# A decoder layer in fp32 on one core: three of eight blocks of the second FFN multiplied with seven products, with the sums of weights made during the first FFN

## The chip, the core and the metric

The kernel runs on one core of a Trainium2 chip. The metric is the device time of one execution in microseconds (us). Before the change the median of three timed runs is 2130.41 us (2130.28 to 2133.94).

## What is computed

The reference is one layer of a decoder trunk on 272 tokens (16 learned ones and 256 of the input), model width 2048, all in float32:

```python
h = h + 0.5 * swiglu(rms_norm(h), w_gate, w_up, w_down)      # first FFN, 5632 wide
u = rms_norm(h); z = u @ w_in                                # q, k, v, index q and k, conv, gates
h = h + (sigmoid(ga) * attention(z) + sigmoid(gc) * conv(z)) @ w_out
h = h + 0.5 * swiglu(rms_norm(h), w_gate2, w_up2, w_down2)   # second FFN, 5632 wide
return h[:, 16:]
```

`swiglu(x) = (silu(x @ w_gate) * (x @ w_up)) @ w_down`. Nearly all the work is matrix products with weights that are read once, about 390 MB in all.

## The kernel before, in words

**Float32 by three products.** Every operand is split into a high and a low part: ScalarE (ACT) writes `hi`, the value rounded to the matmul's type (`nc.scalar.activation(hi, raw, AF.Copy)`, L193), and VectorE (DVE) writes `lo = raw - hi` (L194). A product is hi·hi + hi·lo + lo·hi, so three matmuls. In the second FFN the three stand in `trio` (L431 to L433), 128 by 128 against 128 by 512. I call these three matmuls a trio. In the first FFN they are L397 to L399, 272 columns wide.

**The stream of weights.** The class `Stream` feeds all of it. A load is a DMA that SP issues into a raw buffer (L165). A step is a tile of at most 1024 columns that is split into `whi` and `wlo`; four pairs of these buffers exist, and `next()` hands the matmuls the oldest step after splitting three steps ahead (`AHEAD = 3`). The order of all engines is written out by the program: each call of `next()` runs the functions that are due. `st.put(fn, slot)` makes `fn` due slot // 2 steps later, before that step's split if the slot is even and behind it if it is odd. The table `LAG` holds those slots. `st.later(fn, lag)` does the same counted in whole steps.

**First FFN.** 264 steps, each of them 8 times 3 matmuls, at two steps per raw buffer of 2048 columns (1 MB).

**Second FFN.** Gate and up weights are cut into 11 column blocks f (groups of 6 and 5), each with eight depth blocks i of 2 by 2 sub-blocks; after each group of f, two passes d of the down projection follow, over 12 or 10 depth blocks. An ordinary block i is two steps "0" and "1" of four trios each. A mixed block computes the same 2 by 2 product with seven trios in place of eight (the Winograd form of Strassen's method), for four sums of weights (`t1` to `t4`, L214, four DVE operations of 128 by 512) and some sums of activations (`combos`, made once per operand). Before, blocks 2 and 5 of the eight are mixed (block 5 alone in the first f), and in the down passes blocks 5, 7, 9 of 12 and 5, 7 of 10. Its steps a, b, c, d (2, 2, 2 and 1 trios) are interleaved with the next block's steps, "a 0 b c 1 d", and the sums are made by DVE in between, in the raw buffers and in a tile `mix`. Raw loads of the second FFN go through a ring of six half buffers of 1024 columns (512 KB).

**What follows a block f.** The seven products lie in PSUM banks: four in `c` (one tile `three` of two banks, and `one`, `two`), four more in `m`, which is the other set of banks, and the next f swaps the two sets. After the last mixed block `spread` empties `m` (ACT L757, DVE L758 to L761); at the end of f `gather` empties `c` (DVE L771 to L773), `silu` (L779) and `times` (L786) make the gated value, `turn_gated` transposes 32 by 32 blocks (L658), `move_blocks` sends the tile to DRAM and back (POOL, L666 `hold<-mt` and four of L669 `mt<-hold`), and `split_blocks` writes the high and low part of `mid` (ACT L808, DVE L809), the operand of the down projection. Then `combos` prepares the sums of `mid` for a mixed block (L719 to L723, L705, L706). All these stand in the in-order queues of DVE and ACT between the splits of weights.

Of the kernel before, what the change touches and what calls it, by code (L numbers as in the profile page):

```python
# [15 lines left out]
P = 128  # L16
D = 2048
# [38 lines left out]
AHEAD = 3  # L56
WARM = 4, 4, 1
# [8 lines left out]
MIXED = 2, 5  # L66
FIRST_MIXED = 5,
MADE = ()
JOBS_FROM, JOBS_EVERY = 24, 7
DOWN_MIXED = {6: (5, 7, 9), 5: (5, 7)}  # L70
RAW = 2048
LEAD = dict(t3=3, t1=1, t2=3, t4=1)
LAG = dict(
    spread=(0, 0, 0, 0, 0), gather=(0, 2, 2), silu=(6, 6), times=(6, 8), turn=(11, 11), move=19, hi=(29, 27),
    lo=(29, 28), combos=(32, 32, 32, 32, 32, 32, 32, 37, 37), last_times=(6, 6), last_turn=(7, 7, 9, 9),
    last_split=14, half=(0, 3), drain=(8, 8, 12), act_combos=(6, 29, 30), factors=(10, 12, 14),
    out=(1, 2, 4, 16),
# [3 lines left out]
def order(n, mixed, made=()):  # L81

    out, i = [], 0
    while i < n:
        if i not in mixed:
            out += [(i, "0"), (i, "1")]
        else:
            a, b, c, d = [(i, x) for x in ("ABCD" if i in made else "abcd")]
            if i + 1 in mixed or i + 1 == n:
                out += [a, b, c, d]  # L90
            else:
                i += 1
                out += [a, (i, "0"), b, c, (i, "1"), d]
        i += 1
    return out


class Stream:
# [7 lines left out]
    def __init__(self, nc, raw_pool, split_pool):  # L106
        self.nc, self.raw_pool, self.split_pool = nc, raw_pool, split_pool
        self.loads, self.subs = [], []
        self.raw, self.ready = {}, {}
        self.n_loaded = self.n_split = self.at = 0  # L110
        self.blocks, self.waiting, self.steps = [], [], []
        self.first = []
        self.ring, self.n_ring, self.kept, self.done = [], 0, 0, set()

    def add(self, src, n, width, cuts=()):

        per = min(SUB // width, SUB // P)
        g = len(self.loads)
        self.loads.append((src, n * width, cuts, 2))
        at = [0, *cuts, n] if cuts else [*range(0, n, per), n]  # L120
        for a, b in zip(at, at[1:]):
            view = lambda a=a, b=b: self.raw[g][:, a * width : b * width]
            self.subs.append([view, b - a, width, [g] if b == n else [], []])

    def add_part(self, name, src, made=None):

        def load(x):
            self.loads.append((x, x.shape[1], (), 1))
            return len(self.loads) - 1

        if name in "01ABCD":
            g = load({
                "0": lambda: src[:, :SUB], "1": lambda: src[:, SUB:], "A": lambda: src[:, HALF : 3 * HALF],
                "B": lambda: src[:, 3 * HALF :], "C": lambda: made[:, :SUB], "D": lambda: made[:, SUB:],
            }[name]())
            n = self.loads[g][1]
            self.subs.append([lambda: self.raw[g][:, :n], n // HALF, HALF, [g], []])
        else:
            at = len(self.subs)
            if name == "a":  # L140
                self.pair = load(src[:, :SUB]), load(src[:, SUB:]), at, {}
            one, two, start, own = self.pair
            view = lambda: self.part(self.raw[one], self.raw[two], name)
            self.subs.append([view, 1 if name == "d" else 2, HALF, [], []])
            for x in dict(a=(), b=("t1",), c=("t3", "t2"), d=("t4",))[name]:
                own[x] = max(start, at - LEAD[x])
                self.subs[own[x]][4].append((x, lambda x=x: self.sum_of(self.raw[one], self.raw[two], x)))
            own[name] = at
            if name == "d":
                self.subs[max(own["b"], own["t2"])][3].append(one)  # L150
                self.subs[max(own["a"], own["t4"])][3].append(two)

    def load_one(self, between=(), queues=()):
        src, n, cuts, slots = self.loads[self.n_loaded]
        if slots == 1:
            tile, half = divmod(self.n_ring, 2)
            if tile < RAW_BUFS and not half:
                self.ring.append(self.raw_pool.tile([P, RAW], F32, name="raw"))
            raw = self.ring[tile % RAW_BUFS][:, half * SUB : half * SUB + SUB]
            self.n_ring += 1  # L160
        else:
            raw = self.raw_pool.tile([P, RAW], F32, name="raw")
# [13 lines left out]
    def fill(self):  # L176
        while self.n_loaded < len(self.loads) and (
            sum(x[3] for x in self.loads[self.kept : self.n_loaded + 1]) <= 2 * RAW_BUFS
        ):
            self.load_one()  # L180

    def split(self, upto):
        nc = self.nc
        while self.n_split < min(upto, len(self.subs)):
            view, kk, width, done, sums = self.subs[self.n_split]
# [18 lines left out]
    def blocks_of(self, one, two):  # L204
        b12, b11, b22, b21 = (x[:, i * HALF : (i + 1) * HALF] for x in (one, two) for i in range(2))
        return b12, b11, b22, b21, *(self.mix[:, i * HALF : (i + 1) * HALF] for i in range(3))

    def sum_of(self, one, two, name):

        b12, b11, b22, b21, t3, t2, t4 = self.blocks_of(one, two)  # L210
        to, a, b, op = dict(
            t3=(t3, b22, b12, "sub"), t1=(b12, b12, b11, "sub"), t2=(t2, t3, b11, "add"), t4=(t4, b21, t2, "sub")
        )[name]
        getattr(self.nc.vector, f"tensor_{op}")(to, a, b)  # L214

    def part(self, one, two, name):

        return dict(a=two, b=one, c=self.mix[:, : 2 * HALF], d=self.mix[:, 2 * HALF :])[name]
# [18 lines left out]
    def next(self):  # L237

        if not self.blocks:
            self.run(self.first, self.at)  # L240
            if self.steps:
                self.steps.pop(0)()
            self.split(self.at + 1 + AHEAD)
# [18 lines left out]
def tile_decoder_layer(  # L262
# [53 lines left out]
    for n in GROUPS:  # L316
        for f in range(n):
            now = MIXED if gu else FIRST_MIXED
            sums = {i: scratch.tile([P, RAW], F32, name=f"made{gu + i}") for i in now if i in MADE}
            made += [(gu + i, x) for i, x in sums.items()]  # L320
            for i, name in order(8, now, MADE):
                st.add_part(name, wgu2[gu + i], sums.get(i))
            gu += 8
        for _ in range(2):
            for i, name in order(2 * n, DOWN_MIXED[n]):
                st.add_part(name, wd2[down + i])
            down += 2 * n
# [107 lines left out]
    def quads(c, m, x, mixed, n, after_mixed, tail=False, made=()):  # L435
# [5 lines left out]
        for i, name in order(n, mixed, made):  # L441
# [7 lines left out]
            else:  # L449
# [3 lines left out]
                unit = dict(a=(p3, p2), b=(p5, p1), c=(p7, p6), d=(p4,), A=(p1, p3), B=(p2,), C=(p5, p6), D=(p7, p4))  # L453
                unit = [(*p, b) for b, p in enumerate(unit[name])]
            plan.append((unit, i == max(mixed) and name in "dD"))
# [121 lines left out]
    def ffn_features():  # L577
# [3 lines left out]
        with tc.tile_pool(name="ffn1", bufs=2, reuse_waits="tile") as fp:  # L581
# [16 lines left out]
            def job(i, to, at):  # L598
# [18 lines left out]
            for at, (i, to) in enumerate(made):  # L617
                job(i, to, JOBS_FROM + at * JOBS_EVERY)
# [56 lines left out]
    def ffn_tokens():  # L675

        with ExitStack() as pools:
# [3 lines left out]
            st.mix = fp.tile([P, 3 * HALF], F32, name="mix")  # L681
# [12 lines left out]
            late["junk"] = lambda: u[:, 0]  # L694

# [56 lines left out]
            put((add_up, root, inverse), LAG["factors"])  # L752
# [23 lines left out]
            def silu():  # L776
                s = gate_of()
                return [
                    lambda j=j: nc.scalar.activation(s[:, j - 1], s[:, j - 1], AF.Silu, scale=rcol[:, 0, j - 1 : j])  # L779
# [69 lines left out]
            for g, n in enumerate(GROUPS):  # L849
                for f in range(n):  # L850
                    box = {}
                    x, c, m = banks()
                    if f == g == 0:
                        rest = [i for i in MIXED if i not in FIRST_MIXED]
                        for i, slot in zip((*FIRST_MIXED, *rest), LAG["act_combos"]):
                            put(act_combos(i), 9 * (slot,))
                    now = {i: mixed[i] for i in (MIXED if f or g else FIRST_MIXED)}
                    quads(c, m, lambda k, j, part: known(("act", k // 4), act_tokens(k, j, part)), now, 8, lambda m=m: put(spread(m), LAG["spread"]), made=MADE)
# [717 lines left out]
```

## Time and profile before

| | |
|---|---|
| timed runs, median (lowest to highest) | 2130.41 us (2130.28 to 2133.94) |
| profiled execution: its time, its span | 2132.07 us, 2130.30 us |
| granted clock of the core | 1.00 |
| TensorE (PE) matmul busy | 2118.7 us, 99% |
| VectorE (DVE) busy | 1465.6 us, 69% |
| ScalarE (ACT) busy | 1016.3 us, 48% |
| moved by DMA | 411.28 MB, mean 193 GB/s |
| second FFN, first to last matmul | 1419.2 to 2124.2 us |

Matmuls are pipelined, so their busy times overlap, and a PE that is 99% busy can still have places where one matmul starts late. Such places are seen by counting the matmuls in equal stretches, and in the waits of PE itself. A line of waits reads: engine and line that waited, what released it, total us, times, the longest one. In a line of groups the last field is the idle time of that engine just before these instructions. In a line of windows "x" is the number of instructions that run in the stretch.

### The profile page before, as it was taken

Reading aid. Unit: us, or ns where it says so; the run is one execution under the profiler, and the core shown is the slowest. Engines: PE = TensorE matmul, PEld = TensorE weight load, DVE = VectorE, ACT = ScalarE, POOL = GpSimd, SP = SyncE. Lnnn points to the kernel's source line nnn. Section 1 sums busy time; section 2 is a strip of 40 time slices with the busy share of each in tenths; the row PEclk is TensorE's granted clock in tenths of the full one; section 3 lists DMA queues with packets and bytes.
Section 4 is the critical chain, followed back from the end, with each engine's and each line's share of the span. In section 5 each row is a group of like instructions: output and inputs, shape, how many; then the busy total and the mean of one; then the engine's idle time right before and its main releaser. Section 6 shows DMA issues by size and latency. Waiting matters only on the chain.

```text
span 2130.3 us, 31646 instructions
## 1 busy us (share of the span) xinstructions
PE 2118.7 (99%) x12809; PEld 1903.1 (89%) x12809; DVE 1465.6 (69%) x1953; ACT 1016.3 (48%) x1273; POOL 45.8 (2%) x93
## 2 busy tenths in 40 slices
PE   9999999999999999999999999999999999999999
PEld 9999999999999998799988888888887888888787
DVE  7555544455555556677677477768898887888897
ACT  6444433344444445455544444455555555554553
POOL 0000000000000000000000000010000000000000
PEclk9999999999999999999999999999999999999999
DMA  7555545555555555445455555676676766576664
GB/s 265 188 178 178 178 178 178 178 178 178 179 178 179 178 176 176 171 159 171 160 186 195 197 186 197 220 251 192 221 228 196 225 214 191 190 235 219 216 200 157
DMA packets 80291, 411.28 MB, mean 193 GB/s; under 512 B 9488, under 2 KB 10256, under 8 KB 49680
## 3 DMA queue, kind: packets, MB, share of 16 engines
q1 hardware_dynamic: 74880, 393.52, 54.9%
q0 software_dynamic: 4688, 14.68, 2.1%
q8 instruction: 100, 1.64, 0.3%
q10 hardware_dynamic: 576, 1.05, 0.1%
q14 instruction: 47, 0.39, 0.1%
HBM read 400.30 MB, written 8.91 MB: 192 GB/s over the span
## 4 chain that ended last, share of the span: by engine, by line
PE 88%; issue 7%; DMA 3%; DVE 1%; ACT 1%; POOL 1%; SPq 0%; DVEq 0%; ACTq 0%; POOLq 0%
PE pd L398 4%; PE pd L399 4%; PE pd L397 4%; PE pu L397 4%; PE pg L397 4%; PE pu L398 4%; PE pg L398 4%; PE pg L399 4%; PE pu L399 4%; PE three L431 4%; PE three L433 4%; PE three L432 4%; PE pgt L427 3%; PE pgt L426 3%; PE pgt L425 3%
## 5 line engine op out<-in xcount | busy, mean ns | idle before, releaser
L194 DVE TENSOR_TENSOR wlo<-raw,whi 128x1024 fp32r<-128x1024 f32 (+1 forms) x749 | 909.4, 1219 | 587.2 <-ACT whi L193 581.5
L193 ACT ACTIVATE whi<-raw 128x1024 fp32r<-128x1024 f32 (+1 forms) x749 | 787.6, 1056 | 914.8 <-PE three L433 169.8
L397 PE MATMUL pd<-mid,whi 128*128 128x272 f32 x704 | 201.7, 286 | 0.0
L398 PE MATMUL pd<-mid,whi 128*128 128x272 f32 x704 | 201.7, 286 | 0.0
L399 PE MATMUL pd<-mid,wlo 128*128 128x272 f32 x704 | 201.7, 286 | 0.0
L397 PE MATMUL pu<-act,whi 128*128 128x272 f32 x672 | 192.6, 287 | 0.0
L399 PE MATMUL pu<-act,wlo 128*128 128x272 f32 x672 | 192.5, 287 | 0.0
L397 PE MATMUL pg<-act,whi 128*128 128x272 f32 x672 | 192.5, 286 | 0.0
L398 PE MATMUL pg<-act,whi 128*128 128x272 f32 x672 | 192.5, 286 | 0.0
L399 PE MATMUL pg<-act,wlo 128*128 128x272 f32 x672 | 192.5, 286 | 0.0
L398 PE MATMUL pu<-act,whi 128*128 128x272 f32 x672 | 192.5, 286 | 0.0
L431 PE MATMUL three<-whi,act 128*128 128x512 f32 x352 | 137.2, 390 | 0.9 <-DVE u L761 0.7
L433 PE MATMUL three<-whi,act 128*128 128x512 f32 x352 | 137.0, 389 | 0.0
L432 PE MATMUL three<-wlo,act 128*128 128x512 f32 x352 | 137.0, 389 | 0.0
L397 PEld LDWEIGHTS pd<-mid,whi 128*128 128x128 f32 x704 | 132.6, 188 | 0.0
L398 PEld LDWEIGHTS pd<-mid,whi 128*128 128x128 f32 x704 | 132.6, 188 | 0.0
L399 PEld LDWEIGHTS pd<-mid,wlo 128*128 128x128 f32 x704 | 132.6, 188 | 0.0
L397 PEld LDWEIGHTS pg<-act,whi 128*128 128x128 f32 x672 | 126.6, 188 | 0.0
L399 PEld LDWEIGHTS pu<-act,wlo 128*128 128x128 f32 x672 | 126.6, 188 | 0.0
L398 PEld LDWEIGHTS pg<-act,whi 128*128 128x128 f32 x672 | 126.6, 188 | 0.0
L398 PEld LDWEIGHTS pu<-act,whi 128*128 128x128 f32 x672 | 126.6, 188 | 0.0
L397 PEld LDWEIGHTS pu<-act,whi 128*128 128x128 f32 x672 | 126.5, 188 | 0.0
(333 smaller groups left out, 4296.8 us busy)
## 6 DMA issues: line engine op xcount, KB each, us to landing
raw<-in_wgu_dram SPq DMA_DIRECT2D x177, 512.0 KB, 5.0
raw<-in_wgu_dram SPq DMA_DIRECT2D x86, 1024.0 KB, 4.8
raw<-in_wd_dram SPq DMA_DIRECT2D x44, 1024.0 KB, 4.8
raw<-in_wd_dram SPq DMA_DIRECT2D x88, 512.0 KB, 5.0
raw<-in_wcv_dram SPq DMA_DIRECT2D x24, 1024.0 KB, 4.8
raw<-in_wgc_dram SPq DMA_DIRECT2D x24, 1024.0 KB, 4.8
raw<-in_wga_dram SPq DMA_DIRECT2D x24, 1024.0 KB, 4.9
raw<-in_wo_dram SPq DMA_DIRECT2D x16, 1024.0 KB, 4.8
```

The lines of the kernel that those rows point to most:

```text
L193: nc.scalar.activation(hi[:, :n], raw, AF.Copy)
L194: nc.vector.tensor_sub(lo[:, :n], raw, hi[:, :n].bitcast(F32))
L397: nc.tensor.matmul(ps, whi, xhi, start=first, stop=False)
L398: nc.tensor.matmul(ps, whi, xlo, start=False, stop=False)
L399: nc.tensor.matmul(ps, wlo, xhi, start=False, stop=last)
L425: nc.tensor.matmul(ps, xhi, whi, start=k + i == 0, stop=False)
L426: nc.tensor.matmul(ps, xhi, wlo, start=False, stop=False)
L427: nc.tensor.matmul(ps, xlo, whi, start=False, stop=k + i == n - 1)
L431: nc.tensor.matmul(ps, x(0), w[0], start=first, stop=False)
L432: nc.tensor.matmul(ps, x(0), w[1], start=False, stop=False)
L433: nc.tensor.matmul(ps, x(1), w[0], start=False, stop=last)
```

## The change

1. **Three mixed blocks.** Blocks 1, 3, 5 of the eight are mixed (3 alone in the first f). The down passes keep theirs.
2. **Sums made early.** For each of the 41 mixed blocks (31 of gate and up, 10 of down) a job in the first FFN loads the weights (POOL, 1 MB), makes the four sums in place on DVE, and stores the tile to DRAM (POOL, 1 MB). Jobs start at step 24 and follow each other every 5 steps; a job's four sums come 5 to 8 steps after its load was issued, its store 9 steps after. Three buffers hold the jobs; for the first three a one-column copy on DVE keeps the load from being issued earlier.
3. **New steps.** A mixed block is now steps A, B, C, D (2, 1, 2 and 2 trios). A and B come from three quarters of the weights (1536 columns), C and D from the stored tile (2048 columns). They are not interleaved with the next block. The sums, the tile `mix` and the ring of half buffers are gone.
4. **Raw loads** of the second FFN fill whole buffers of 2048 columns; three buffers as before, and one is free when all its steps are split.
5. **Five pairs of split buffers** in the second FFN, and four steps ahead.
6. **Other places** in `LAG`: `gather` at once (0, 0, 0), `silu` 1, `times` 2, `turn` 4, `move` 12, `hi` 27, `combos` from 29 to 36, the factors of the norm at 23 to 27, and others.

```diff
-MIXED = 2, 5
-FIRST_MIXED = 5,
-JOBS_FROM, JOBS_EVERY = 24, 7
+MIXED = 1, 3, 5
+FIRST_MIXED = 3,
+JOBS_FROM, JOBS_EVERY = 24, 5
 LAG = dict(
-    spread=(0, 0, 0, 0, 0), gather=(0, 2, 2), silu=(6, 6), times=(6, 8), turn=(11, 11), move=19, hi=(29, 27),
+    spread=(0, 0, 0, 1, 1), gather=(0, 0, 0), silu=(1, 1), times=(2, 2), turn=(4, 4), move=12, hi=(27, 27),
...
-            a, b, c, d = [(i, x) for x in ("ABCD" if i in made else "abcd")]
-            if i + 1 in mixed or i + 1 == n:
-                out += [a, b, c, d]
-            else:
-                i += 1
-                out += [a, (i, "0"), b, c, (i, "1"), d]
+            out += [(i, x) for x in "ABCD"]
...
+        if name in "0A":
+            self.own = load(src if name == "0" else src[:, HALF:]), name == "A" and load(made)
+        g = self.own[name in "CD"]
+        a, b = {"0": (0, 2), "1": (2, 4), "A": (0, 2), "B": (2, 3), "C": (0, 2), "D": (2, 4)}[name]
...
-        while self.n_loaded < len(self.loads) and (
-            sum(x[3] for x in self.loads[self.kept : self.n_loaded + 1]) <= 2 * RAW_BUFS
-        ):
+        while self.n_loaded < min(len(self.loads), self.kept + RAW_BUFS):
             self.load_one()
...
-            for _, fn in sorted(sums, key=lambda x: ("t3", "t1", "t2", "t4").index(x[0])):
-                fn()
...
-            hi = self.split_pool.tile([P, SUB], F32R, name="whi")
-            lo = self.split_pool.tile([P, SUB], F32R, name="wlo")
+            hi, lo = self.place()
...
             for i, name in order(2 * n, DOWN_MIXED[n]):
-                st.add_part(name, wd2[down + i])
+                st.add_part(name, wd2[down + i], sums.get(i))
...
                 def load():
                     box["x"] = fp.tile([P, RAW], F32, name="made", bufs=3)
-                    nc.gpsimd.dma_start(box["x"], wgu2[i])
+                    if at < JOBS_FROM + 3 * JOBS_EVERY:
+                        nc.vector.tensor_copy(box["x"][:, :1], ones[:, :1])
+                    nc.gpsimd.dma_start(box["x"], src)
...
+            st.more = [[fp.tile([P, SUB], F32R, name=f"{n}{i}") for n in ("whi", "wlo")] for i in range(MORE)]
+            st.ahead = AHEAD + MORE
```

The function `job` stood in the kernel before, with an empty list of blocks.

**How the order of DVE changes at the end of a block f of the second FFN.** Before, from the last rows of one f's `spread` (L758 to L761) to the `gather` (L771 to L773) and the first sum of weights (L214) of the next:

```order
L194 TENSOR_TENSOR wlo<-raw,whi 128x1024 x2
L758 TENSOR_TENSOR u<-one,u 128x512
L759 TENSOR_TENSOR u<-two,u 128x512
L760 TENSOR_TENSOR u<-three,u 128x512
L761 TENSOR_TENSOR u<-three,u 128x512
L194 TENSOR_TENSOR wlo<-raw,whi 128x1024
L706 TENSOR_TENSOR below<-few,below 128x3x128
L194 TENSOR_TENSOR wlo<-raw,whi 128x1024
L771 TENSOR_TENSOR few<-three,u 128x1024
L194 TENSOR_TENSOR wlo<-raw,whi 128x1024
L772 TENSOR_TENSOR u<-one,u 128x512
L214 TENSOR_TENSOR mix<-raw 128x512
```

The `spread` stands two splits ahead of the next `gather`, and sums of weights stand among the splits. The same place on DVE with the change; L722 to L725 are the `spread`, L735 to L737 the `gather`, L161 the split:

```order
L670 TENSOR_TENSOR below<-few,below 128x3x128
L722 TENSOR_TENSOR u<-one,u 128x512
L723 TENSOR_TENSOR u<-two,u 128x512
L161 TENSOR_TENSOR wlo<-raw,whi 128x1024
L724 TENSOR_TENSOR u<-three,u 128x512
L725 TENSOR_TENSOR u<-three,u 128x512
L161 TENSOR_TENSOR wlo<-raw,whi 128x1024 x2
L161 TENSOR_TENSOR wlo_14193<-raw,whi_14192 128x512
L735 TENSOR_TENSOR few<-three,u 128x1024
L736 TENSOR_TENSOR u<-one,u 128x512
L737 TENSOR_TENSOR u<-two,u 128x512
L161 TENSOR_TENSOR wlo<-raw,whi 128x1024
```

Four splits now stand between the two, and no sum of weights is left; the whole `gather` comes in one piece.

**SP's loads at the start of the second FFN**, before and with the change (`in_wo` is the weight of the projection ahead of it, `in_wgu` the gate and up weights, `made_74` the stored tile of the first job):

```order
L165 DMA raw<-in_wo_dram 128x2048 x16
L165 DMA raw<-in_wgu_dram 128x1024 x96
L165 DMA raw<-in_wd_dram 128x1024 x48
L165 DMA raw<-in_wgu_dram 128x1024 x80
L165 DMA raw<-in_wd_dram 128x1024 x40
```

```order
L137 DMA raw<-in_wo_dram 128x2048 x16
L137 DMA raw<-in_wgu_dram 128x2048 x3
L137 DMA raw<-in_wgu_dram 128x1536
L137 DMA raw<-made_74 128x2048
L137 DMA raw<-in_wgu_dram 128x2048 x5
L137 DMA raw<-in_wgu_dram 128x1536
L137 DMA raw<-made_75 128x2048
```

Equal half loads become whole ones, and a mixed block loads one and three quarters of what an ordinary one loads.

More of the change, by code (lines that the diff above doesn't have):

```diff
@@ L56 @@
 AHEAD = 3
+MORE = 1
 WARM = 4, 4, 1
@@ L65, with order @@
 HALF = 512
-MIXED = 2, 5
-FIRST_MIXED = 5,
-MADE = ()
-JOBS_FROM, JOBS_EVERY = 24, 7
+MIXED = 1, 3, 5
+FIRST_MIXED = 3,
+JOBS_FROM, JOBS_EVERY = 24, 5
 DOWN_MIXED = {6: (5, 7, 9), 5: (5, 7)}
 RAW = 2048
-LEAD = dict(t3=3, t1=1, t2=3, t4=1)
 LAG = dict(
-    spread=(0, 0, 0, 0, 0), gather=(0, 2, 2), silu=(6, 6), times=(6, 8), turn=(11, 11), move=19, hi=(29, 27),
-    lo=(29, 28), combos=(32, 32, 32, 32, 32, 32, 32, 37, 37), last_times=(6, 6), last_turn=(7, 7, 9, 9),
-    last_split=14, half=(0, 3), drain=(8, 8, 12), act_combos=(6, 29, 30), factors=(10, 12, 14),
-    out=(1, 2, 4, 16),
+    spread=(0, 0, 0, 1, 1), gather=(0, 0, 0), silu=(1, 1), times=(2, 2), turn=(4, 4), move=12, hi=(27, 27),
+    lo=(28, 28), combos=(29, 29, 32, 32, 33, 33, 36, 36, 36), last_times=(4, 6), last_turn=(8, 11, 14, 14),
+    last_split=16, half=(1, 5), drain=(1, 3, 3), act_combos=(4, 7, 26), factors=(23, 25, 27), out=(1, 2, 4, 17),
+    act_split=(6, 15, 31),
 )
-def order(n, mixed, made=()):
+def order(n, mixed):
     out, i = [], 0
@@ L112, in __init__ @@
         self.first = []
-        self.ring, self.n_ring, self.kept, self.done = [], 0, 0, set()
+        self.kept, self.done = 0, set()
+        self.more, self.turn, self.ahead = [], 0, AHEAD
     def add(self, src, n, width, cuts=()):
@@ L118, in add @@
         g = len(self.loads)
-        self.loads.append((src, n * width, cuts, 2))
+        self.loads.append((src, n * width, cuts))
         at = [0, *cuts, n] if cuts else [*range(0, n, per), n]
@@ L122, in add @@
             view = lambda a=a, b=b: self.raw[g][:, a * width : b * width]
-            self.subs.append([view, b - a, width, [g] if b == n else [], []])
+            self.subs.append((view, b - a, width, (g,) if b == n else ()))
     def add_part(self, name, src, made=None):
         def load(x):
-            self.loads.append((x, x.shape[1], (), 1))
+            self.loads.append((x, x.shape[1], ()))
             return len(self.loads) - 1
[L131 to L151, printed above, removed]
@@ L153, in load_one @@
-    def load_one(self, between=(), queues=()):
[L154 to L162, printed above, removed]
+        if name in "0A":
+            self.own = load(src if name == "0" else src[:, HALF:]), name == "A" and load(made)
@@ L163, in load_one @@
+        g = self.own[name in "CD"]
+        a, b = {"0": (0, 2), "1": (2, 4), "A": (0, 2), "B": (2, 3), "C": (0, 2), "D": (2, 4)}[name]
+        self.subs.append((lambda: self.raw[g][:, a * HALF : b * HALF], b - a, HALF, (g,) if name in "1BD" else ()))
+    def load_one(self, between=(), queues=()):
+        src, n, cuts = self.loads[self.n_loaded]
+        raw = self.raw_pool.tile([P, RAW], F32, name="raw")
         at = [0, *(c * P for c in cuts), n]
@@ L202, in split, with place @@
             self.fill()
[L204 to L218, printed above, removed]
+    def place(self):
+        if self.more:
+            self.turn = (self.turn + 1) % (SPLIT_BUFS + len(self.more))
+            if self.turn < len(self.more):
+                return self.more[self.turn]
+        return [self.split_pool.tile([P, SUB], F32R, name=n) for n in ("whi", "wlo")]
     def put(self, fn, slot):
@@ L242, in next @@
                 self.steps.pop(0)()
-            self.split(self.at + 1 + AHEAD)
+            self.split(self.at + 1 + self.ahead)
             self.run(self.waiting, self.at)
@@ L318, in tile_decoder_layer @@
             now = MIXED if gu else FIRST_MIXED
-            sums = {i: scratch.tile([P, RAW], F32, name=f"made{gu + i}") for i in now if i in MADE}
-            made += [(gu + i, x) for i, x in sums.items()]
-            for i, name in order(8, now, MADE):
+            sums = {i: scratch.tile([P, RAW], F32, name=f"made{gu + i}") for i in now}
+            made += [(wgu2[gu + i], x) for i, x in sums.items()]
+            for i, name in order(8, now):
                 st.add_part(name, wgu2[gu + i], sums.get(i))
@@ L324, in tile_decoder_layer @@
         for _ in range(2):
+            sums = {i: scratch.tile([P, RAW], F32, name=f"sums{down + i}") for i in DOWN_MIXED[n]}
+            made += [(wd2[down + i], x) for i, x in sums.items()]
             for i, name in order(2 * n, DOWN_MIXED[n]):
-                st.add_part(name, wd2[down + i])
+                st.add_part(name, wd2[down + i], sums.get(i))
             down += 2 * n
@@ L433, in trio, with quads @@
         nc.tensor.matmul(ps, x(1), w[0], start=False, stop=last)
-    def quads(c, m, x, mixed, n, after_mixed, tail=False, made=()):
+    def quads(c, m, x, mixed, n, after_mixed, tail=False):
         def of(k, j):
@@ L440, in quads @@
         plan, joined = [], []
-        for i, name in order(n, mixed, made):
+        for i, name in order(n, mixed):
             k = 2 * i
@@ L452, in quads @@
                 p5, p6, p7 = (m[5], s1), (m[6], s2), (m[7], s3)
-                unit = dict(a=(p3, p2), b=(p5, p1), c=(p7, p6), d=(p4,), A=(p1, p3), B=(p2,), C=(p5, p6), D=(p7, p4))
+                unit = dict(A=(p1, p3), B=(p2,), C=(p5, p6), D=(p7, p4))
                 unit = [(*p, b) for b, p in enumerate(unit[name])]
-            plan.append((unit, i == max(mixed) and name in "dD"))
+            plan.append((unit, i == max(mixed) and name == "D"))
         flat = [id(p[0]) for unit, _ in plan for p in unit]
@@ L596, in times, with job @@
                 nc.vector.tensor_mul(box["v"], box["v"], box["s"])
-            def job(i, to, at):
+            def job(src, to, at):
                 box = {}
@@ L615, in job @@
                 st.later(lambda: nc.gpsimd.dma_start(to, box["x"]), at + JOBS_EVERY + 4)
-            for at, (i, to) in enumerate(made):
-                job(i, to, JOBS_FROM + at * JOBS_EVERY)
+            for i, (src, to) in enumerate(made):
+                job(src, to, JOBS_FROM + i * JOBS_EVERY)
             two = [aux_tile(f"start{i}") for i in range(2)]
@@ L679, in ffn_tokens @@
             mid = fp.tile([P, 4 * GROUPS[0], 2, SEQ], F32R, name="mid")
-            st.mix = fp.tile([P, 3 * HALF], F32, name="mix")
             u = fp.tile([P, 4, 512], F32, name="u")
@@ L750, in add_up @@
                 nc.vector.tensor_add(sums[:, 0], sums[:, 0], sums[:, 2])
-            put((add_up, root, inverse), LAG["factors"])
+            put((add_up, root, lambda: (inverse(), written.add("rcol"))), LAG["factors"])
             def spread(m):
@@ L778, in silu @@
                 return [
-                    lambda j=j: nc.scalar.activation(s[:, j - 1], s[:, j - 1], AF.Silu, scale=rcol[:, 0, j - 1 : j])
+                    lambda j=j: nc.scalar.activation(s[:, j - 1], s[:, j - 1], AF.Silu, scale=known("rcol", rcol[:, 0, j - 1 : j]))
                     for j in (1, 2)
@@ L854, in ffn_tokens @@
                         rest = [i for i in MIXED if i not in FIRST_MIXED]
-                        for i, slot in zip((*FIRST_MIXED, *rest), LAG["act_combos"]):
-                            put(act_combos(i), 9 * (slot,))
+                        for i, *slots in zip((*FIRST_MIXED, *rest), LAG["act_combos"], LAG["act_split"]):
+                            put(act_combos(i), 5 * (slots[0],) + 4 * (slots[1],))
                     now = {i: mixed[i] for i in (MIXED if f or g else FIRST_MIXED)}
-                    quads(c, m, lambda k, j, part: known(("act", k // 4), act_tokens(k, j, part)), now, 8, lambda m=m: put(spread(m), LAG["spread"]), made=MADE)
+                    quads(c, m, lambda k, j, part: known(("act", k // 4), act_tokens(k, j, part)), now, 8, lambda m=m: put(spread(m), LAG["spread"]))
                     put(gather(x, c), LAG["gather"])
```

2 lines of the change are left out of this document (1 added, 1 removed).

## The prediction

> **What bounds the kernel now.** I read the page first, then the second FFN in equal stretches, the waits of PE, ACT and DVE there, the chain of waits, the groups by line, and the DMAs' times to landing.
>
> The page's parts 1 and 4, busy time by engine and the chain that ended last:
>
> ```profile
> span 2130.3 us, 31646 instructions
> PE 2118.7 (99%) x12809; PEld 1903.1 (89%) x12809; DVE 1465.6 (69%) x1953; ACT 1016.3 (48%) x1273; POOL 45.8 (2%) x93
> PE 88%; issue 7%; DMA 3%; DVE 1%; ACT 1%; POOL 1%; SPq 0%; DVEq 0%; ACTq 0%; POOLq 0%
> ```
>
> The chain is PE nearly throughout: the end moves when PE has fewer matmuls, or when places vanish where it waits. What a trio costs is seen in the chain by its pieces inside the second FFN, the first matmuls (L431) of two trios in a row:
>
> ```profile
> 1466.64 0.23 PE two L431
> 1467.32 0.23 PE three L431
> ```
>
> They start 0.68 us apart, 0.2267 us per matmul. In stretches (us, PE busy and matmuls, PEld, DVE, ACT, POOL, clock, DMA share, GB/s), the first FFN, the end of the projection ahead of the second FFN, the whole second FFN, and three pieces of it:
>
> ```profile
> 95.00:700.00 605.00, 605.00 (x4908) 605.00 (x4907) 315.58 (x380) 243.33 (x287) 0.32 (x1) 1.00 0.51 179
> 1350.00:1419.00 69.00, 69.00 (x306) 57.11 (x305) 43.74 (x56) 35.04 (x50) 8.43 (x15) 1.00 0.76 258
> 1419.60:2124.20 704.60, 699.24 (x3069) 574.72 (x3068) 596.07 (x726) 365.94 (x405) 29.70 (x54) 1.00 0.65 208
> 1620.00:1660.00 40.00, 38.75 (x169) 31.12 (x168) 35.29 (x46) 21.19 (x25) 0.56 (x1) 1.00 0.69 216
> 1720.00:1760.00 40.00, 40.00 (x178) 33.14 (x177) 31.17 (x33) 19.53 (x20) 0.00 (x0) 1.00 0.74 235
> 1960.00:2000.00 40.00, 38.17 (x166) 30.56 (x165) 35.09 (x47) 20.48 (x25) 0.56 (x1) 1.00 0.66 207
> ```
>
> Undisturbed, 40 us hold 178 matmuls; at the ends of the two groups of gate and up they hold 169 and 166, so 9 and 12 are missing, 2.0 and 2.7 us. By the program the second FFN has 1025 trios, 1025 x 0.68 = 697.0 us, and it takes 704.6: **7.6 us are lost in it.** What PE, and ACT ahead of it, wait for there:
>
> ```profile
> PE one L432 <- DVE wlo L194: 3.7, 7, 0.8
> PE three L431 <- DVE u L761: 1.1, 3, 0.4
> ACT whi L193 <- PE three L433: 224.1, 183, 2.3
> ACT mid L808 <- DMA mt<-hold: 30.4, 9, 4.8
> ACT whi L193 <- DMA raw<-in_wgu_dram: 0.8, 2, 0.6
> ```
>
> PE waits for a late split on DVE or for `spread`, never for DMA itself. The weights come in time: ACT waits 224 us for PE to free a buffer and 0.8 us for a raw load. But ACT also stands 30.4 us in all before the tile that returns from DRAM, with splits queued behind. The chain shows where this reaches PE:
>
> ```profile
> 1652.27 7.45 DMA hold<-mt
> 1660.25 1.64 POOL mt L669 x3
> 1661.88 5.45 DMA mt<-hold
> 1668.60 0.52 ACT mid L808
> 1674.79 1.22 DVE wlo L194
> 1677.97 0.69 DVE u L761
> 1678.80 0.47 PE three L431
> ```
>
> The tile lands at 1667, then splits, `combos` and `spread` follow on a DVE with no room left, and PE's first matmul of the down pass starts late.
>
> **Part by part.** *Fewer trios.* 31 mixed blocks of gate and up in place of 21: ten trios less, 30 matmuls, 10 x 0.68 = **6.8 us off PE**. This is certain as work; the rest decides whether it shows.
>
> *Sums leave the second FFN.* Groups by line on DVE in the second FFN, and the split in the first:
>
> ```profile
> L194 DVE TENSOR_TENSOR wlo<-raw,whi 128x1024 fp32r<-128x1024 f32 x261 | 316.2, 1221 | 55.5 <-ACT whi L193 51.0
> L214 DVE TENSOR_TENSOR mix<-mix,raw 128x512 f32<-128x512 f32 x31 | 21.5, 692 | 1.1
> L786 DVE SCALAR_TENSOR_TENSOR few<-u,rcol,few 128x512 f32<-128x512 f32 x22 | 16.2, 746 | 0.0
> L771 DVE TENSOR_TENSOR few<-three,u 128x1024 f32<-128x1024 f32 x11 | 13.4, 1218 | 0.0
> L772 DVE TENSOR_TENSOR u<-one,u 128x512 f32<-128x512 f32 x11 | 7.5, 684 | 0.0
> L194 DVE TENSOR_TENSOR wlo<-raw,whi 128x1024 fp32r<-128x1024 f32 x205 | 251.4, 1227 | 288.2 <-ACT whi L193 288.2
> ```
>
> 31 mixed blocks x 4 sums x 0.69 = 85 us leave a DVE that is busy 596 of 704.6; the ten new ones add 10 splits of 1024 and 10 of 512 columns, 10 x (1.22 + 0.68) = 19 us on DVE (less on ACT, which has 339 us free). So 596 - 85 + 19 = 530 us of 698, 76% instead of 85%. In a mixed pair DVE had 3 x 1.22 + 0.68 + 2.76 of sums + 2.45 = 9.5 us to do in 15 trios or 10.2 us; now 6.8 us. The seven late splits sit in those pairs, so I expect most to go. The three waits for `spread` (L761) go too: before, step d of block 5 came with only block 7's eight trios (5.4 us) ahead of the next f; now D has blocks 6 and 7 behind it, 10.9 us.
>
> *The round trip through DRAM.* It takes 16 us from the turn: 7.45 + 1.64 + 5.45 in the chain above and the issues between. The turn's own row:
>
> ```profile
> L658 DVE STREAM_TRANSPOSE mt<-few 128x512 f32<-128x512 f32 x18 | 11.7, 687 | 0.0
> ```
>
> Before, the turn is due at slot 11, behind a split that waits for 18 trios of the next f: 12.2 + 2.3 + 1.4 = 15.9 us, so the tile is back at 31.9. The first `hi`, slot 27, stands behind a split that waits for 41 trios: 27.9 + 1.1 = 29.0. ACT would wait 2.9 us; measured are 30.4 / 9 = 3.4, so the method holds. Now the turn ends 8 us after the end of f (on DVE 2.6 of `gather`, 1.2 of split, 1.5 of `times`, 1.2, 1.4), the tile is back at 24, and ACT reaches `hi` after 34 trios and a split, 23.1 + 1.1 = 24.2. The wait falls from 3.4 us to between 0 and 2.
>
> Together the 7.6 us lost shrink to between 0 and all of it. I take 2.6, nearer to the free end, since each named cause is eased: **5.0 us off**.
>
> *The same work in the first FFN.* 41 x 4 x 0.69 = 113 us go to DVE there, where it idles 288.2 of 605 us for ACT; a step is 605 / (4908 / 24) = 2.96 us of PE, holding 1.23 us of split and now four sums in five steps, 0.55. Cover remains: splits run three steps ahead, 8.9 us. POOL's queue gains 82 DMAs, 2 x 1.05 MB per 14.8 us, 142 GB/s on top of 179. What the engines can do, at the start of the program and later, in stretches:
>
> ```profile
> 15.00:20.00 5.00, 4.67 (x38) 4.46 (x38) 4.28 (x8) 4.45 (x11) 0.00 (x0) 1.00 1.03 428
> 17.00:23.00 6.00, 6.00 (x51) 6.00 (x50) 5.67 (x10) 6.00 (x15) 0.00 (x0) 1.00 0.94 367
> 150.00:156.00 6.00, 6.00 (x51) 6.00 (x50) 3.60 (x5) 2.52 (x4) 0.00 (x0) 1.00 0.52 175
> ```
>
> 428 GB/s were moved, above the 321 needed, and PE runs 51 matmuls in 6 us at 367 GB/s as at 175. So heavier traffic alone doesn't slow PE; I cost this part at nothing (if the cover fails, below). No load of 1 MB by POOL is in the trace; nearest are these issues (KB, median us to landing), and below them SP's raw loads in the second FFN:
>
> ```profile
> raw<-in_wgu_dram SPq DMA_DIRECT2D x86, 1024.0 KB, 4.8
> hold<-mt POOLq DMA_DIRECT2D x10, 512.0 KB, 7.4
> mt<-hold POOLq DMA_DIRECT2D x40, 128.0 KB, 5.3
> DMA to landing us min/median/max: 3.4/5.0/8.4
> ```
>
> Between 4.8 and 2 x 7.4 = 14.8 us, and the sums ask for it 5 steps, 14.8 us, after its issue. I take 7.4: nothing waits. The Trainium skill, page "DMA: Bandwidth & Descriptors", section "Bandwidth", gives 6.15 us for 1 MB issued from GpSimd; by that, too, the sum would keep a zero here.
>
> *Whole raw buffers.* A mixed and an ordinary block load 0.79 + 1.05 + 1.05 = 2.88 MB in 10.2 us: 283 GB/s, near the 258 at the end of the projection, where PE lost nothing. A buffer is free when its last step is split. The tightest one carries C and D of block 3: its buffer held C and D of block 1, whose last split ends 6.7 us after f began (`gather` 2.6, splits 2 x 1.22, `times` 1.5, and 0.2). Issue 0.5 and landing 4.8 make 12.0; PE needs C after 26 trios, 17.7 us, less 2.3 for its two halves of the split: 15.4. So 3.4 us are left, and the load may take 8.2 us. Waits of ACT for raw will appear; PE should not see them.
>
> *Fifth pair of buffers, other slots of the norm's factors and of the first `combos`:* nothing, since ACT and DVE have time; the fifth pair is what keeps C and D, short steps, ahead.
>
> **Sum.** The profiled execution took 2132.07 us, 1.77 around its span of 2130.30; the median of the timed runs, 2130.41, lies 1.66 below. I work on the span and put the difference onto the median: -6.8 - 5.0 = -11.8, so 2130.41 - 11.8 = **2118.6 us**. With no loss left in the second FFN: 2130.4 - 6.8 - 7.6 = 2116.0.
>
> **Rivals.** *The lost time stays* (only the trios count). For: the end of a group still has the same chain of `gather`, transposes and round trip, and more DMA traffic can take back the slot's margin. Against: DVE's 85 us. 2130.4 - 6.8 = 2123.6, from 2121.5 to 2126.
>
> *Raw loads too late (slower).* For: 283 GB/s through three buffers, largest landing seen 8.4 us with half the size. Against: the median of 4.8 for 1 MB in every stage, and that splits which come late no longer wait for PE, so buffers free faster. It decides above 8.2 us of landing. At 10 us the C and D loads of blocks 3 and 5 each cost 1.8 us in ten f: 2 x 10 x 1.8 = 36, so 2116.0 + 36 = 2152. Slower than before from 2130.4 on: 14.4 / 20 = 0.7 us beyond, so at 8.9 us.
>
> *Jobs too late (slower).* A sum waits in DVE's queue, with the splits behind it, for a POOL load, and POOL's load i+2 stands behind store i. Two jobs have 29.6 us; sums 2.8, store and issues 1.0 leave about 25.8 for a load. Beyond that each us costs one for each of 20 pairs; at 30 us it is 20 x 4.2 = 84, so 2118.6 + 84 = 2203 us. Against: 5.3 and 7.4 us were measured with DVE 85% busy. The Trainium skill, page "SBUF — State Buffer", section "SBUF: two separate sides", says that GpSimd can't write the descriptors of its DMAs while a DVE operation in a two-port mode holds the port that they share, and its next section has a DMA that takes five times as long for it. By that rule a load could take 5 x 7.4 = 37 us and the time go to 2343; the landings beside a busy DVE don't bear it out here.
>
> *The change does less than it says:* the trios are gone but new waits of 7 us or more eat them; 2130.
>
> **How the numbers follow.** Chances: forecast 0.62 (2116 to 2121.5), lost time stays 0.23, raw loads late 0.08, jobs late 0.03, eaten 0.04. A measurement of this kernel tells about 0.2% (4.3 us) from no change, so faster means under 2126.1: 0.62 + 0.23 and a little of the rest, 0.86; the same 0.04; slower 0.10. The range runs from 2115.6, all lost time gone and a little, to 2125.5, nearly all of the first rival.
>
> **What would show it.** Right: PE's matmuls in the second FFN 30 fewer and its stretch about 693 us; waits of L431 and L432 for DVE near zero; ACT's wait for `mt<-hold` under 10 us; the first FFN's stretches with 4908 matmuls in 605 us as before, DVE near 70% there. Wrong: PE waiting for `whi` or `wlo` behind raw loads that land later than 8.2 us; a first FFN longer than before; DVE waits for the jobs' loads; fewer than 178 matmuls in 40 us at the ends of the groups.

## The result and the profile after

The changed kernel takes 2121.27 us (2119.97 to 2122.30, four runs) against 2130.73 of the kernel before in the same comparison: a ratio of 0.995, 95% interval 0.9935 to 0.9965. The prediction was 2118.6 us, with a range from 2115.6 to 2125.5; the stretch that it gave to its main case, 2116 to 2121.5, ends 0.2 us above what came.

The page of the changed kernel, span, busy time and chain:

```profile
span 2119.5 us, 31665 instructions
PE 2110.2 (100%) x12779; PEld 1897.8 (90%) x12779; DVE 1503.4 (71%) x2023; ACT 1027.4 (48%) x1295; POOL 89.0 (4%) x175
PE 91%; DMA 4%; DVE 3%; issue 1%; ACT 1%; SPq 0%; DVEq 0%; ACTq 0%
```

PE has 30 matmuls less, and DMA and DVE have a larger part of the chain. The second FFN is measured from its first matmul to its last. The last one of before, then both of the changed kernel (start us, us, engine, line):

```profile
2125.19 0.39 PE L433 MATMUL two<-whi,mid 128*128 128x512 f32 x1
```

```profile
1419.05 0.39 PE L392 MATMUL one<-whi,act 128*128 128x512 f32 x1
2113.89 0.39 PE L394 MATMUL two<-whi,mid 128*128 128x512 f32 x1
```

Before it ran from 1419.17 (the row after the projection's last) to 2125.58, the end of that last matmul and not 2124.2, so 706.4 us, with 697.2 of matmuls (3075 at 226.7 ns): 9.2 us lost. Now it runs 695.2 us with 690.4 of matmuls: **4.8 us lost**. It starts at the same time, so all of the gain is here: 6.8 us of matmuls and 4.4 us of waits, 11.2 us in the two traces. The medians are 9.5 us apart, since the profiled execution of before, 2132.07 us, lies 1.3 above its median and that of the changed kernel does not. Stretches of the changed kernel: the first FFN, and pieces of the second:

```profile
95.00:700.00 605.00, 605.00 (x4907) 605.00 (x4907) 411.74 (x541) 243.11 (x287) 42.05 (x80) 1.00 0.86 318
1460.00:1500.00 40.00, 39.57 (x175) 32.32 (x174) 31.23 (x36) 24.09 (x28) 2.76 (x5) 1.00 0.85 294
1500.00:1540.00 40.00, 40.00 (x178) 33.14 (x177) 31.15 (x34) 23.27 (x27) 2.74 (x5) 1.00 0.82 284
1580.00:1620.00 40.00, 39.34 (x174) 32.26 (x173) 31.30 (x37) 22.97 (x27) 2.73 (x5) 1.00 0.82 282
1900.00:1940.00 40.00, 39.21 (x172) 31.95 (x171) 32.43 (x35) 24.02 (x27) 2.73 (x5) 1.00 0.79 275
```

The first FFN holds its matmuls at 318 GB/s. In the second, the stretches with fewer than 178 matmuls no longer lie only at the ends of the groups. The rate of the loads alone doesn't mark them: 1500 to 1540 holds all 178 at 284 GB/s. Who waits now, PE and then ACT in the second FFN:

```profile
PE one L393 <- DVE wlo L161: 2.5, 5, 0.8
ACT whi L160 <- PE three L394: 162.3, 113, 2.8
ACT whi L160 <- DMA raw<-in_wgu_dram: 57.3, 31, 5.3
ACT whi L160 <- DMA raw<-made: 35.5, 17, 3.0
```

ACT's 30.4 us before the tile back from DRAM are gone; in their place it waits 93 us for raw loads, 0.8 us before. The chain of the changed kernel at the first of PE's five waits, and below it the raw loads' times to landing in the second FFN:

```profile
1475.14 1.07 ACT whi L160
1476.23 1.24 DVE wlo L161
1477.49 10.05 DMA raw<-made
1487.64 1.07 ACT whi L160
1488.73 1.01 DVE wlo L161
1489.88 0.88 DVE wlo L161
...
1491.01 1.29 DVE mid L773 x2
1492.30 1.15 DVE wlo L161
1493.49 0.50 PE one L393
```

```profile
DMA to landing us min/median/max: 4.1/5.4/11.2
```

The load of C and D of block 5 goes out when a buffer is free (1476.23 and 1.24) and takes 10.05 us. Behind it come the splits of C and D, the two pieces of `mid`, and the split of block 6's first step, for which PE waits at 1493.49. Two of the five waits have this chain. The other three stand behind the load of block 4, an ordinary one; the longest of them, with PE's matmul at 1903.46:

```profile
1891.31 9.67 DMA raw<-in_wgu_dram
1901.09 1.07 ACT whi L160
1902.18 1.24 DVE wlo L161
```

In the microseconds of the first chain POOL issues the four returns of the round trip:

```profile
1475.47 0.56 POOL L632 DMA_DIRECT2D mt<-hold  x1 [5.17 <-DMA hold<-mt]
1476.21 0.55 POOL L632 DMA_DIRECT2D mt<-hold  x1 [0.18 <-issue]
1477.90 1.09 POOL L632 DMA_DIRECT2D mt<-hold  x2 [1.14 <-issue]
```

### The profile page after: what moved, and what is told of

It reads as the page before. It is cut to its first block, busy times and chain, and to the rows that moved or that the text cites. A ratio compares the mean times of both kernels' runs of the same rounds, so it can differ in the third digit from the quotient of the medians.

```text
span 2119.5 us, 31665 instructions
## 1 busy us (share of the span) xinstructions
PE 2110.2 (100%) x12779; PEld 1897.8 (90%) x12779; DVE 1503.4 (71%) x2023; ACT 1027.4 (48%) x1295; POOL 89.0 (4%) x175
## 4 chain that ended last, share of the span: by engine, by line
PE 91%; DMA 4%; DVE 3%; issue 1%; ACT 1%; SPq 0%; DVEq 0%; ACTq 0%
PE three L393 4%; PE three L394 4%; PE three L392 4%; PE pd L359 4%; PE pd L360 4%; PE pd L358 4%; PE pu L358 4%; PE pg L358 4%; PE pu L359 4%; PE pg L359 4%; PE pg L360 4%; PE pu L360 4%; PE pgt L386 3%; PE pgt L388 3%; PE pgt L387 3%; DMA raw<-made 2%
## 5 line engine op out<-in xcount | busy, mean ns | idle before, releaser
L161 DVE TENSOR_TENSOR wlo<-raw,whi 128x1024 fp32r<-128x1024 f32 (+1 forms) x831 | 978.7, 1191 | 577.1 <-ACT whi L160 574.0
L160 ACT ACTIVATE whi<-raw 128x1024 fp32r<-128x1024 f32 (+1 forms) x831 | 848.1, 1033 | 983.3 <-PE three L394 162.3
## 6 DMA issues: line engine op xcount, KB each, us to landing
made<-in_wgu_dram POOLq DMA_DIRECT2D x31, 1024.0 KB, 10.6
```

The lines of the kernel that those rows point to most:

```text
L160: nc.scalar.activation(hi[:, :n], raw, AF.Copy)
L161: nc.vector.tensor_sub(lo[:, :n], raw, hi[:, :n].bitcast(F32))
```

## The experiments

Ratios are against the kernel before in the same comparison (medians of 2131.15 to 2131.74 us), with a 95% interval, also where the edit is made on the changed kernel.

**1. The trios alone.** On the kernel before:

```diff
-MIXED = 2, 5
-FIRST_MIXED = 5,
+MIXED = 1, 3, 5
+FIRST_MIXED = 3,
```

> The kernel before with blocks 1, 3, 5 mixed in place of 2, 5, its sums still made by VectorE in the second FFN. My theory (sums have to leave VectorE for the trios to show): per block f VectorE then has three pairs of 9.5 us, two ordinary blocks of 2.45 and some 10 us besides, 43 us, against 41.5 us of TensorE, so TensorE waits 2 to 3 us more in each of ten f; 6.8 us of matmuls less, 20 to 30 us of waits more: 2140 to 2155 us. Rival (only the trios count): 2123.6 us.

Measured: 2162.25 us, ratio 1.0143 (1.0125 to 1.0162). Its second FFN takes 735.5 us, 45 lost. PE's waits in it, and then ACT's:

```profile
PE one L432 <- DVE wlo L194: 16.2, 23, 1.3
PE two L432 <- DVE wlo L194: 5.5, 9, 0.8
...
ACT whi L193 <- DVE raw L214: 69.0, 20, 4.5
```

ACT's waits for sums made in the raw buffers (L214) were 14.4 us before. So DVE is what holds up the mixed pairs, as my theory had it, and by more than it said (20 to 30 us). With its sums and places as before, the third mixed block costs far more than its 6.8 us.

**2 and 3. The sums alone.** On the kernel before; the second version has the copy that holds back the first three job loads:

```diff
-MADE = ()
+MADE = 2, 5
...
                     box["x"] = fp.tile([P, RAW], F32, name="made", bufs=3)
+                    if at < JOBS_FROM + 3 * JOBS_EVERY:
+                        nc.vector.tensor_copy(box["x"][:, :1], ones[:, :1])
```

> The kernel before with the sums of gate and up made early for its own two mixed blocks, places and half loads as before. My theory: VectorE loses 21 x 2.76 = 58 us in the second FFN and the late splits in mixed pairs go, but the round trip through DRAM is as late as before (3.4 us of ScalarE waiting each time); 2 to 4 us of the 7.6 lost come back: 2126.5 to 2128.5 us. Rival (the sums on VectorE were covered): 2130.5 us. Second rival (jobs in the first FFN cost time): above 2132 us and a first FFN longer than 781 us.

> The kernel before with the sums of its two mixed blocks made early, as in the run that gained 4.6 us in the second FFN and lost 5.9 ahead of it, now with the one-column copy that holds back the first three job loads. Theory (the loss came from those three loads at the very start): the second FFN starts at 1419 us again and takes about 702 us: 2125 to 2127 us. Rival (jobs every 7 steps cost the first FFN time): 2129 us or more.

Measured: without the copy 2133.49 us, ratio 1.0011 (1.0002 to 1.0020), no gain where I forecast 2 to 4 us; with it 2127.40, ratio 0.9977 (0.9967 to 0.9987). The second FFN takes 701.8 and 703.2 us, so 4.6 and 6.0 us are lost there in place of 9.2, but without the copy it starts at 1425.1. The sums bring 3 to 5 us by themselves. PE's waits for `spread` are gone in both, those for late splits fall from 3.7 us to 1.1 and 1.9, and ACT's for the tile from DRAM from 30.4 to 16.8 and 19.1.

**4. The copy alone.** On the changed kernel:

```diff
-                    if at < JOBS_FROM + 3 * JOBS_EVERY:
-                        nc.vector.tensor_copy(box["x"][:, :1], ones[:, :1])
```

> The changed kernel without the one-column copy that holds back the first three job loads. Theory (three loads of 1 MB by GpSimd at the very start delay the first weights, which is what the kernel before with early sums lost): the second FFN starts 4 to 7 us later and the time is 2125 to 2128.5 us. Rival (that loss came from the first FFN's jobs themselves): 2121.3 us.

Measured: 2127.26 us, ratio 0.9977 (0.9966 to 0.9988). The stretch from 10 to 20 us without the copy (us, PE busy with its matmuls, then clock and GB/s at the end):

```profile
10.00:20.00 10.00, 6.68 (x40) 6.46 (x41) 6.06 (x11) 6.93 (x13) 0.00 (x0) 0.83 1.02 410
```

PE's wait at the start, in the same run (us in all, count, the longest):

```profile
PE start L358 <- ACT whi L160: 3.8, 1, 3.8
```

In the changed kernel the same stretch has 80 matmuls at 423 GB/s and a clock of 1.00. Without the copy POOL issues two job loads of 1 MB from 1.3 us on (the third stands in its queue behind the first store, at 98.9), and the raw loads issued in the first 20 us land after 10.3 us at the median in place of 5.5. PE waits 3.8 us and goes on at a lower clock, and the second FFN starts at 1424.7, 5.7 us later. The jobs themselves cost nothing at one in five steps, but this line, which looks like a detail, is worth 5 to 6 us.

**5. Two mixed blocks.** On the changed kernel:

```diff
-MIXED = 1, 3, 5
-FIRST_MIXED = 3,
+MIXED = 2, 5
+FIRST_MIXED = 5,
```

> The changed kernel with blocks 2 and 5 mixed as before (5 alone in the first f), all else as changed. My theory: ten trios come back, 10 x 0.68 = 6.8 us, and there are fewer raw loads to be late: 2125.5 to 2128 us. Rival (the gain is in places and sums, the trios were hidden): 2121 us.

Measured: 2122.62 us, ratio 0.9954 (0.9940 to 0.9969). Its first and last matmul in the second FFN are at 1419.32 and here:

```profile
2116.09 0.39 PE L394 MATMUL two<-whi,mid 128*128 128x512 f32 x1
```

697.2 us, exactly its 3075 matmuls, and PE has no wait there at all. I had forecast 2125.5 to 2128. So all of the change but the third block (sums, places, loads and buffers together) gives back the whole 9.2 us, and the third mixed block, with 6.8 us of matmuls less, costs 4.8 us of new waits: it is worth 2 in the traces. The timed ratios, 0.9954 and 0.9950, don't tell the two kernels apart.

**6 and 7. The places.** On the changed kernel, first nearly all slots of before, then those of `silu`, `times` and `turn` alone:

```diff
-    spread=(0, 0, 0, 1, 1), gather=(0, 0, 0), silu=(1, 1), times=(2, 2), turn=(4, 4), move=12, hi=(27, 27),
+    spread=(0, 0, 0, 0, 0), gather=(0, 2, 2), silu=(6, 6), times=(6, 8), turn=(11, 11), move=19, hi=(29, 27),
```

```diff
-silu=(1, 1), times=(2, 2), turn=(4, 4)
+silu=(6, 6), times=(6, 8), turn=(11, 11)
```

> The changed kernel with the slots of before (gather, silu, times, turn, hi, combos, spread, factors and the rest), only those that empty the banks of the down passes kept new, since a mixed block 1 needs them early. My theory: the turn is late again, ScalarE waits about 3 us for each round trip, and lost time goes back from 3 us towards 7: 2123.5 to 2126.5 us. Rival (the places do nothing, room on VectorE does all): 2121.3 us.

> The changed kernel with only the slots of silu, times and turn as before (6, 6 and 8, 11), so that the gated tile goes out to DRAM about three steps, 5 to 6 us, later; hi still asks for it at slot 27. Theory (the place of the turn carries what the old places cost): ScalarE waits 4 to 6 us in each of nine round trips, some 40 to 50 us in all, and TensorE loses 20 to 40 us: 2136 to 2160 us. Rival (other slots, spread, gather or combos, did it): 2121 to 2128 us.

In the second, the last f of each group has its `times` ahead of `silu`, so these two blocks compute other values with the same instructions. Measured: 2160.40 us, ratio 1.0129 (1.0112 to 1.0146), and 2166.58, ratio 1.0152 (1.0114 to 1.0189). I had expected 2123.5 to 2126.5 of the first and 2136 to 2160 of the second. ACT's wait for the tile with the old places:

```profile
ACT mid L772 <- DMA mt<-hold: 60.2, 9, 8.8
```

PE in the timeline of the same run, at the first matmul behind one of these waits:

```profile
1497.80 0.79 PE L392 MATMUL one<-whi,act 128*128 128x512 f32 x1 [5.13 <-ACT whi L160]
```

The two stretches around it (PE's matmuls, and the granted clock third from the end):

```profile
1490.00:1500.00 10.00, 4.40 (x15) 2.99 (x14) 3.06 (x5) 3.83 (x5) 0.00 (x0) 0.79 0.67 217
1500.00:1510.00 10.00, 10.00 (x40) 8.04 (x39) 9.32 (x11) 5.30 (x7) 0.00 (x0) 0.87 0.64 202
```

Steps are shorter now (22 in a block f, 20 before), so the same slots ask for the tile earlier. Each round trip leaves ACT 6.7 us, and PE up to 5.1 us, without work. And then PE runs slow: the matmul behind the wait takes 0.79 us and not 0.39, the granted clock is 0.79 and 0.87 in those stretches. The Trainium skill, page "TensorE: Matmul & The Clock Gate", Part 1, says that the clock is halved after an idle window of about 3.4 us until PE has been busy for another; the row agrees. But shorter waits did it too: from 1640 to 1650, around one of 2.4 us, the granted clock is 0.66. The clock fell behind seven of the nine waits. PE's own waits in the second FFN:

```profile
PE one L392 <- ACT whi L160: 25.0, 9, 5.1
PE one L393 <- DVE wlo L161: 6.1, 9, 0.8
```

So 31 of the 51 us lost are waits. The mean granted clock of 0.97 over the 741.7 us of this second FFN makes about 20 us more, by estimate. The second version has the same waits (52.9 us in nine), so the late turn, with its `silu` and `times`, carries the cost, and the other slots little of it.

**8. No round trip.** On the changed kernel, with the tile's way through DRAM left out:

```diff
-                        st.put(lambda box=box: move_blocks(box["x"]), LAG["move"])
```

> The changed kernel without the round trip of the gated tile through DRAM (the operand of the down projection is then taken from the tile as it lies, in the wrong order). Left out: ten hold and forty return DMAs. First theory (the raw loads of C and D land late, near 10 us, because the return's 128 KB pieces run at the same time): TensorE's waits in the second FFN, 4.9 us lost, fall to 1 or less: 2116.5 to 2118 us. Second theory (three raw buffers are too few for 283 GB/s by themselves): 3 us or more stay lost: 2119.5 to 2121 us.

Measured: 2116.48 us, ratio 0.9931 (0.9916 to 0.9946). The second FFN takes 690.5 us and PE has no wait in it. The raw loads:

```profile
DMA to landing us min/median/max: 4.1/4.9/7.8
```

Nine trips are gone here; the one near 1429 us, ahead of the first block's end, stays. Without them no load takes over 7.8 us, and PE waits for none, with the same three buffers and 283 GB/s from 1460 to 1500. Whether it is the bytes of the trip or its small pieces that stretch the loads is not shown.

**9. Half loads.** On the changed kernel, the ring of six half buffers of before, one load for each step:

```diff
-        if name in "0A":
-            self.own = load(src if name == "0" else src[:, HALF:]), name == "A" and load(made)
+        g = load({
+            "0": lambda: src[:, :SUB], "1": lambda: src[:, SUB:], "A": lambda: src[:, HALF : 3 * HALF],
+            "B": lambda: src[:, 3 * HALF :], "C": lambda: made[:, :SUB], "D": lambda: made[:, SUB:],
+        }[name]())
```

> The changed kernel with the raw loads of the second FFN through a ring of six half buffers of 1024 columns as before, one load for each of the steps 0, 1, A, B, C, D. Both theories of late loads: a half is free as soon as its one step is split, so a load may take some 8 us and not 5 to 8; lost time falls from 4.9 us to between 1 and 3: 2117.5 to 2119.5 us. Rival (whole buffers are what keeps the loads in time): 2122 us or more.

Measured: **2116.00 us**, ratio 0.9929 (0.9914 to 0.9944), the lowest median of all, under every run of the changed kernel (2115.65 to 2116.61 against 2119.97 to 2122.30) and under the 2117.5 that I had as the least. A stretch of its second FFN:

```profile
1460.00:1500.00 40.00, 40.00 (x179) 33.10 (x178) 31.89 (x36) 24.75 (x28) 2.76 (x5) 1.00 0.89 293
```

Its raw loads there:

```profile
DMA to landing us min/median/max: 2.9/5.5/10.7
```

Loads still take up to 10.7 us beside the round trip. They go out earlier, though, since a half is free as soon as its one step is split (the stored tile of the chain above at 1474.65 in place of 1477.49), and PE waits for nothing in the 690.5 us.

**10 and 11. Buffers.** On the changed kernel, four pairs of split buffers; then four pairs and a fourth raw buffer in their room:

```diff
-MORE = 1
+MORE = 0
...
+            st.more_raw = [fp.tile([P, RAW], F32, name="raw4")]
```

> The changed kernel with four pairs of split buffers and three steps ahead in the second FFN, as before. My theory: the pair is the cover that raw loads of 8 to 10 us need; without it each late load costs one step more, 0.7 to 2.7 us, in most of ten f: lost time 10 to 20 us, 2126 to 2137 us. Rival (the pair does nothing): 2121.3 us.

> Four raw buffers of 2048 columns in the second FFN and four pairs of split buffers: the room of the fifth pair is given to a raw buffer. Theory (late raw loads are what is left): loads go out one buffer, about 3.8 us, earlier than with three, no load is late, and the time is well under that with four pairs and three raw buffers: 2116 to 2121 us. Rival (the splits' lead is what is short): as with four pairs alone, within 2 us.

Measured: 2121.15 us, ratio 0.9950 (0.9934 to 0.9967), with four pairs: no difference to five in the time, and 2126 to 2137 was expected. With the fourth raw buffer 2116.86, ratio 0.9933 (0.9919 to 0.9948), a second FFN of 690.4 us without a wait of PE. So it is the raw loads that are late; the lead of the splits is not what is short.

**12. A fourth mixed block.** On the half loads: blocks 1, 3, 4, 6, four pairs, a job every 4 steps. Its slots let one block's activation sums overwrite another's before they are split, so it computes other values:

```diff
-MIXED = 1, 3, 5
+MIXED = 1, 3, 4, 6
-JOBS_FROM, JOBS_EVERY = 24, 5
+JOBS_FROM, JOBS_EVERY, JOBS_LEAD = 24, 4, 6
```

> The half loads of the earlier run and blocks 1, 3, 4, 6 mixed (3 alone in the first f), four pairs of split buffers for room, 51 jobs every 4 steps with sums 6 steps after the load, hi, lo and combos two slots later. Ten trios less than with three: 2116.0 - 6.8 = 2109.2 us. Theory (half loads have room left, and the first FFN takes 179 + 177 = 356 GB/s): 2109 to 2112 us. Rival (the loads or the jobs are late now, 309 GB/s in a block f with the round trip): 2114 us or more, with waits for raw loads or for the jobs' loads in the trace.

Measured: 2172.76 us, ratio 1.0186 (1.0157 to 1.0215), the rival. The first FFN in two stretches:

```profile
95.00:700.00 605.00, 569.58 (x4483) 563.33 (x4482) 386.18 (x528) 214.00 (x256) 48.07 (x91) 0.98 0.89 319
700.00:760.00 60.00, 57.02 (x446) 56.40 (x445) 39.56 (x54) 23.93 (x31) 4.56 (x9) 0.97 0.92 338
```

What DVE waits for there:

```profile
DVE made L584 <- DMA made<-in_wgu_dram: 161.7, 35, 6.6
DVE made L584 <- DMA made<-in_wd_dram: 53.5, 10, 7.3
```

The second FFN starts at 1477.3, 58 us late. The 356 GB/s that such jobs ask for don't come: 319 and 338 do, little more than the 318 that the changed kernel already moves. This doesn't show that the DMA engines can give no more. What POOL's next job waits for, in its queue, is that a store lands and frees one of the three buffers (us, times):

```profile
DMA made<-made: 497.2, 41
DMA sums<-made: 74.7, 6
```

A store takes 12.4 us to landing here, 7.5 in the changed kernel. A run with a fourth job buffer would tell the two apart; there is none. The second FFN takes 691.3 us with 683.6 of matmuls, so the fourth block gains nothing there either.

## Why the prediction was right, point by point

- **30 matmuls, 6.8 us:** gone, as counted.
- **The waits of before.** I put them at 7.6 us and 2.6 left. Measured to the true last matmul, they were 9.2, and 4.8 are left: 4.4 us off where I had 5.0. The two errors, 1.6 us too little lost before and 2.2 too little left, nearly cancel, and that is luck; -6.8 - 4.4 = -11.2 against the -11.8 of the sum, and -9.5 by the medians. Another 0.2 us, and the time would have been in the range of the first rival, "the lost time stays", from 2121.5 on.
- **Their causes.** With the sums alone the waits for `spread` vanish and those for late splits fall to about a half or less. The wait for the round trip goes with the earlier turn: none is left with it, 52.9 us of ACT's are there with the old one on the changed kernel. With two mixed blocks nothing is lost; how much of that the loads and buffers give is not separated.
- **The round trip's clock.** ACT's wait was to fall to between 0 and 2 us; the waits list it no more. The price of missing it I had as a few us; on the changed kernel it is 51 to 56, some 30 of waits and the rest, by the estimate above, of PE's lower clock behind most of them.
- **"PE should not see them"** is the step that failed. I gave a load of C and D 8.2 us and took 4.8. The tightest one by my count, C and D of block 3, was right: it landed after 4.7 to 5.8 us in all ten f. Late were the loads of blocks 4 and 5, which I didn't work out. They took up to 11.2 us, where the return through DRAM falls on the same microseconds, a coincidence that I left out. In the one f of the ten with no trip beside it the stored tile of block 5 lands after 5.0 us, and without any trip 7.8 us is the longest and nothing is lost. The rival had loads of 10 us for C and D of blocks 3 and 5. It was right for block 5 and didn't name block 4, and its 36 us were far too much: PE waits in five places, for about 1 us each. The sum left 2.6 us lost, put down to the old causes; 4.8 us are lost, and the chains show raw loads ahead of the late splits.
- **Jobs in the first FFN at nothing:** right for the place of the jobs, with the one-column copy; 605 us hold 4907 matmuls, DVE is 68% busy. But I sized their landing at 7.4 us, and the engines at 428 GB/s. The rows of the changed kernel:

```profile
made<-in_wgu_dram POOLq DMA_DIRECT2D x31, 1024.0 KB, 10.6
made<-made POOLq DMA_DIRECT2D x31, 1024.0 KB, 7.5
```

  10.6 us is inside the bounds of 4.8 and 14.8, with 4 us of cover, and the longest, 13.3, with 1.5; nothing is near the 37 us of the rival "jobs too late". Loads and stores together moved 318 GB/s on average and at most 384 in a stretch of 10 us (420 to 430, DMA share 1.00), so the 428 of loads alone was too much to count on.
- **The job loads at the start:** I passed over the copy in one clause of the description and priced it nowhere; it holds 5 to 6 us.
- **The fifth pair,** "what keeps C and D, short steps, ahead", does nothing that the runs can tell.

## What to carry to other kernels

Work that is taken off the bound engine shows only as far as its feeders keep up: here everything but the third block gave 9.2 us of waits back, and the third block's 6.8 us came through whole only with half loads or a fourth raw buffer. Before trusting a load's median time to landing, look at which other transfers run in the same microseconds, and take the longest one beside those. When steps of a hand-written order get shorter, every slot that hides a fixed time has to be counted again.

## What the runs showed of the hardware that was not expected

- Behind a wait of PE of 5.1 us matmuls take 0.79 us in place of 0.39, and two stretches of 10 us that hold 46 otherwise have 15 and 40. The granted clock fell behind seven of the nine waits of that run, three of them of 1.2 to 2.4 us.
- Raw loads take up to 7.8 us without the round trip; beside its four returns issued by GpSimd the longest of a block f took 8.2 to 11.2 us.
- The DMA engines moved 423 GB/s of loads alone at the start. With stores to DRAM among them they moved 318 on average, and at most 384 over 10 us, then at a DMA share of 1.00.
